# Cached keys turned by VectorE, longer runs of small tilings and 512-column memory matmuls in a streaming encoder step

## The chip, the cores and the metric

One core of one Trainium2 chip runs the whole step. The metric is the device time of one execution in microseconds; a kernel's time is the median of several runs. All data is float32. Most products are made in three passes: each operand is split into a high and a low part in a rounded float32 format (fp32r), and high x high, high x low and low x high are summed. Products with cached keys and values run on plain float32 operands, which the trace shows as two passes per matmul.

## The reference

Two layers over two groups of frames: a prompt of 512 frames, and 8 running streams of 16 frames each with a past of 256 (640 rows of 1024 in all).

```
m_l = rms_normalize(mem) * g_mem[l];  k, v = split(m_l @ w_x_kv[l])     # memory keys and values, 256 x 1024 each
layer 0:  q, k, v, f, gate = split(rmsnorm(x) @ w_fox_in)               # 16 heads of 64
          s = q k^T / 8 + cum(logf)_q - cum(logf)_k ; causal            # k, v: the cache, then the new rows
          x += ((softmax(s) v) * sigmoid(gate)) @ w_fox_out
layer 1:  c_q, c_kv, k_r = split(rmsnorm(x) @ w_mla_a)                  # latent of 256, rotary key of 32
          k_nope, v = split(c_kv @ w_kvb) ; s = (q_nope k_nope^T + q_rope k_r^T) * scale ; chunk mask
          x += (softmax(s) v) @ w_mla_out
each:     x += cross_attn(rmsnorm(x), k_mem, v_mem) ; x += swiglu(rmsnorm(x))
y = rmsnorm(x) * g_final
```

The outputs are y of both groups, the new keys, values and forget logs, the latents, the rotary keys and the memory keys and values.

## The kernel before

The phases follow each other: the first (Fox) attention, cross attention, feed-forward, the latent attention, cross attention, feed-forward. Each phase is written as lists of small steps, and `merge` interleaves several lists by their relative position, so that TensorE finds projections (a "fill" list) between the steps of an attention. A scheduler then orders the instructions on each engine, and engines work their queues in order. DMAs are issued by SyncE.

Weights come through `load_w`: a raw tile of 1024 columns (two buffers) is loaded, ScalarE rounds it into `whi` (L150), VectorE makes the rest `wlo` (L151), three buffers each.

The Fox phase runs over eight pairs of heads. `prompt_list` makes scores, softmax, transposed probabilities and values for the prompt. `sample_list` does it for the running streams in two halves `bq` of four streams: `load` fetches a tile `kr` of 128 x 8 x 128 cached keys (L654) and values `vr`, `keys` turns the keys by TensorE transposes into PSUM (L664, 16 per pair of heads) and VectorE or ScalarE copies them out (L668, L670), `scores` makes four matmuls in column tiles of 32 (L685), `trans` turns the probabilities, `values` makes twelve matmuls in the same tiling (L710), and `turn` brings the result to the output rows. In pairs 6 and 7 the fill is `mem_list`, the memory keys and values of both layers: per head and side 256 columns, two row tiles of 24 matmuls.

The latent phase absorbs the key weights into the queries (`turn_w`, L1488; `absorb`, L1498), then runs over eight pairs of heads of the prompt with the eight running streams spread among them: `keys` turns the cached latent (L1530) and the rotary key (L1535). `up_list` (L1588) takes the streams' results back to value space; `values` of the prompt (L1637) uses column tiles of 64. PSUM has two buffers for scores (`ps_s`), two for transposes (`ps_t`), one for values (`ps_o`) and three for projections (`mm`).

## Time and profile before

| | |
|---|---|
| median of 3 runs | 2115.81 us (2113.45 to 2122.21) |
| profiled execution | 2118.55 us, span 2116.8 us |
| TensorE busy | 2066.9 us, 98% |
| VectorE busy | 1393.1 us, 66% |
| ScalarE busy | 900.0 us, 43% |
| GpSimd busy | 176.0 us, 8% |
| DMA | 234.33 MB in 279279 packets |

The profiled execution is one run under the hardware profiler; its span runs from the first to the last instruction. Busy is the time in which at least one instruction of the engine was in work. Matmuls overlap each other in the array, so the duration of one is longer than its share of the queue.

### The profile page before, as it was taken

What the parts mean: (1) busy time and instruction counts of PE and PEld (TensorE: products, weight loads), DVE (VectorE), ACT (ScalarE), POOL (GpSimd) and SP (SyncE); (2) the same over time, 40 slices, a digit from 0 to 9 for tenths busy, and PEclk for the clock granted to TensorE, in tenths of its full rate; (3) what the DMA queues carried; (4) which work ended last, traced back from release to release, by engine and by line L of the source; (5) the groups of instructions that cost most, each with busy time, mean ns of one, the idle gap of its engine ahead of it and who ended that gap; (6) DMA issues with size and microseconds to landing.
All of it is one profiled execution on the core that took longest, in us unless ns stands there. A gap on an engine that the chain in (4) does not pass through costs nothing. (4 is left out here: it accounts for less than half of the span.)

```text
span 2116.8 us, 35888 instructions
## 1 busy us (share of the span) xinstructions
PE 2066.9 (98%) x14189; PEld 1857.4 (88%) x14189; DVE 1393.1 (66%) x2695; ACT 900.0 (43%) x1793; POOL 176.0 (8%) x362
## 2 busy tenths in 40 slices
PE   7999999999999999999999999999999999999998
PEld 7988888889987899999998978887887799999997
DVE  4454555564646796686686567767546896686686
ACT  4444444454443453343344455554443453343342
POOL 1121212120100000000001301100100000000000
PEclk9999999999999999999999999999999999999999
DMA  7443434477555322232221331112554322232221
GB/s 225 130 137 107 139 112 130 147 230 224 166 165 172 100 72 83 85 91 79 81 80 50 92 95 39 53 44 77 164 167 157 100 74 84 83 92 79 80 81 60
DMA packets 279279, 234.33 MB, mean 111 GB/s; under 512 B 15668, under 2 KB 255924, under 8 KB 279112
## 3 DMA queue, kind: packets, MB, share of 16 engines
q1 hardware_dynamic: 279112, 232.05, 36.0%
q8 instruction: 112, 1.84, 0.4%
q14 instruction: 55, 0.45, 0.1%
HBM read 214.80 MB, written 17.21 MB: 110 GB/s over the span
## 5 line engine op out<-in xcount | busy, mean ns | idle before, releaser
L204 PE MATMUL mm<-hT,whi 128*128 128x320 f32 x1744 | 291.5, 313 | 3.8 <-ACT hT L222 3.8
L204 PEld LDWEIGHTS mm<-hT,whi 128*128 128x128 f32 x1744 | 260.9, 188 | 9.8 <-ACT hT L222 5.2
L151 DVE TENSOR_TENSOR wlo<-raw,whi 128x1024 fp32r<-128x1024 f32 (+4 forms) x145 | 170.1, 1176 | 144.2 <-ACT whi L150 84.8
L318 DVE TENSOR_TENSOR X<-mm,X 128x512 f32<-128x512 f32 x270 | 182.8, 686 | 123.1 <-PE mm L204 121.8
L150 ACT CAST whi<-raw 128x1024 fp32r<-128x1024 f32 (+4 forms) x145 | 144.6, 1002 | 150.8 <-PE mm L204 103.4
L204 PE MATMUL mm<-whi,oT 128*128 128x512 f32 x544 | 182.9, 410 | 1.9 <-DVE X L318 1.1
L1103 ACT CAST whi<-tw 128x512 fp32r<-128x512 f32 (+1 forms) x120 | 91.9, 765 | 213.7 <-PE mm L204 127.5
L204 PE MATMUL mm<-whi,aT 128*128 128x512 f32 x560 | 173.0, 390 | 0.3 <-ACT aT L1068 0.3
L204 PE MATMUL mm<-hT,wlo 128*128 128x320 f32 x872 | 156.8, 312 | 0.0
L204 PEld LDWEIGHTS mm<-hT,wlo 128*128 128x128 f32 x872 | 133.4, 188 | 3.2 <-issue 3.1
L204 PE MATMUL mm<-whi,hT 128*128 128x256 f32 (+2 forms) x800 | 127.5, 298 | 2.4 <-ACT whi L150 1.5
L204 PE MATMUL mm<-s,whi 128*128 128x320 f32 x768 | 128.2, 309 | 0.0
L204 PEld LDWEIGHTS mm<-whi,aT 128*128 128x128 f32 x560 | 104.4, 188 | 22.6 <-ACT aT L1068 1.2
L232 POOL TENSOR_SCALAR rstd<-ss 128x1 f32<-128x1 f32 x49 | 17.2, 352 | 1266.0 <-ACT hn L230 1261.5
L204 PEld LDWEIGHTS mm<-whi,oT 128*128 128x128 f32 x544 | 96.6, 189 | 23.2 <-issue 3.7
L204 PEld LDWEIGHTS mm<-whi,hT 128*128 128x128 f32 x800 | 110.0, 193 | 7.7 <-issue 3.9
L204 PEld LDWEIGHTS mm<-s,whi 128*128 128x128 f32 x768 | 116.6, 188 | 0.0
L1104 DVE TENSOR_TENSOR wlo<-tw,whi 128x512 fp32r<-128x512 f32 (+1 forms) x120 | 103.4, 862 | 18.9 <-ACT whi L1103 18.4
L204 PE MATMUL mm<-wlo,oT 128*128 128x512 f32 x272 | 109.1, 401 | 0.0
L204 PE MATMUL mm<-wlo,aT 128*128 128x512 f32 x280 | 108.8, 389 | 0.0
L1103 ACT CAST whi<-raw 128x1024 fp32r<-128x1024 f32 x44 | 46.3, 1052 | 131.7 <-PE mm L204 72.3
L204 PE MATMUL ps_s<-whi,aT 128*128 128x512 f32 x320 | 98.6, 389 | 0.0
(340 smaller groups left out, 4280.5 us busy)
## 6 DMA issues: line engine op xcount, KB each, us to landing
rawg<-w_ffn_gu SPq DMA_DIRECT2D x80, 512.0 KB
raw<-w_ffn_down SPq DMA_DIRECT2D x44, 512.0 KB
raw<-w_x_kv SPq DMA_DIRECT2D x32, 512.0 KB
kr<-cache_mem_k SPq DMA_DIRECT2D x64, 256.0 KB
vr<-cache_mem_v SPq DMA_DIRECT2D x32, 512.0 KB
raw<-w_fox_in SPq DMA_DIRECT2D x30, 512.0 KB
kr<-cache_fox_k SPq DMA_DIRECT2D x16, 512.0 KB
vr<-cache_fox_v SPq DMA_DIRECT2D x16, 512.0 KB
```

Of the source, the lines that this page charges most:

```text
L150: A.copy(hi[:, 0:m], raw[:, 0:m])
L151: V.tensor_tensor(lo[:, 0:m], raw[:, 0:m], hi[:, 0:m].bitcast(F32), ALU.subtract)
L204: T.matmul(st["ps"][:, 0:n], lhsT=l, rhs=r, start=(j == 0), stop=(j == m - 1))
L232: G.tensor_scalar(r, ss, EPS, None, ALU.add)
L318: V.tensor_tensor(xs, ps, xs, ALU.add)
L1103: A.copy(hi[:, o:o + m], src)
L1104: V.tensor_tensor(lo[:, o:o + m], src, hi[:, o:o + m].bitcast(F32), ALU.subtract)
```

## The change

The cached keys are no longer transposed by TensorE. They are loaded in pieces of 32 columns onto 32 partitions each, so that a 32x32 block transpose on VectorE leaves them turned: four DMAs instead of one for each half pair in the Fox phase, and in the latent phase eight more per stream, which load the latent rows a second time (the first copy is still used as values). The new rows' key copy and the block mask of the probabilities move from VectorE to GpSimd. In the Fox phase both halves of the streams are scored and weighted in one step each; the prompt's last two query tiles of the latent phase share a score block, and its values and `up_list` are made in longer runs. The absorbed key weights are handled in full 128 rows, with the queries' other half set to zero. The memory keys and values are made 512 columns at a time, with the weights asked for in units of two row blocks, one unit ahead.

```diff
-        for h in range(4):
+        for c0 in range(0, D, 512):
             for i in range(2):
-                c0 = i * D + h * XD
                 u = {}
-                def load(u=u, c0=c0):
-                    u["w"] = load_w([(0, XD, w_kv[:, c0:c0 + XD])])
-                    u["row"] = pool().tile([P, 2, XD], F32, tag="mrow", name="mrow", bufs=2)
-                def store(u=u, i=i, h=h):
-                    S.dma_start(outs[i][:, :, h * XD:(h + 1) * XD], u["row"])
-                    S.dma_start(kvd[l][i].rearrange("(t p) n -> p t n", p=P)[:, :, h * XD:(h + 1) * XD], u["row"])
-                L = [load]
-                for t in range(2):
-                    L += gemm(lambda u=u, t=t: as_ops(d["mT"], slice(t * P, (t + 1) * P), u["w"], slice(0, XD), KD),
-                              XD, lambda ps, u=u, t=t: A.copy(u["row"][:, t, :], ps[:, 0:XD]), parts=2)
+                def load(m, u=u, c=i * D + c0):
+                    if m == 0:
+                        u["row"] = pool().tile([P, 2, 512], F32, tag="mrow", name="mrow", bufs=2)
+                    u[m] = load_w([(0, 512, w_kv[:, c:c + 512])], k0=2 * m, kt=2, per=2)
+                def part(m, u=u):
+                    for t in range(2):
+                        if m == 0:
+                            u["ps", t] = psum_mm()
+                        ops = [(d["mT"][ai][:, 2 * m + k, t * P:(t + 1) * P], u[m].get(wi, k))
+                               for wi, ai in PASSES for k in range(2)]
+                        for n, (l, r) in enumerate(ops):
+                            T.matmul(u["ps", t], lhsT=l, rhs=r, start=(m == 0 and n == 0), stop=(m == 3 and n == 5))
+                        if m == 3:
+                            A.copy(u["row"][:, t, :], u["ps", t])
+                def store(u=u, i=i, c0=c0):
+                    S.dma_start(outs[i][:, :, c0:c0 + 512], u["row"])
+                    S.dma_start(kvd[l][i].rearrange("(t p) n -> p t n", p=P)[:, :, c0:c0 + 512], u["row"])
+                L = [lambda load=load: load(0)]
+                for m in range(4):
+                    if m < 3:
+                        L.append(lambda load=load, m=m: load(m + 1))
+                    L.append(lambda part=part, m=m: part(m))
                 groups.append(L + [store])
...
-                    d["kr"] = fp.tile([P, 8, P], F32, tag="kr", name="kr", bufs=1)
-                    S.dma_start(d["kr"], ck[:, 8 * bq:8 * bq + 8, pr * P:(pr + 1) * P])
-                    d["vr"] = fp.tile([P, 8, P], F32, tag="vr", name="vr", bufs=2)
-                    S.dma_start(d["vr"], cv[:, 8 * bq:8 * bq + 8, pr * P:(pr + 1) * P])
-                    d["KT"] = fp.tile([P, 4, KS], F32, tag="KT", name="KT", bufs=2)
-                    V.tensor_copy(d["KT"][:, :, PAST:KS],
+                    kr = d["kr", bq] = fp.tile([P, 32, 32], F32, tag="kr", name="kr", bufs=2)
+                    for i in range(4):
+                        c0 = pr * P + 32 * i
+                        S.dma_start(kr[32 * i:32 * i + 32], ck[:, 32 * bq:32 * bq + 32, c0:c0 + 32])
+                    d["vr", bq] = fp.tile([P, 8, P], F32, tag="vr", name="vr", bufs=2)
+                    S.dma_start(d["vr", bq], cv[:, 8 * bq:8 * bq + 8, pr * P:(pr + 1) * P])
+                    d["KT", bq] = fp.tile([P, 4, KS], F32, tag="KT", name="KT", bufs=3)
+                    G.tensor_copy(d["KT", bq][:, :, PAST:KS],
                                   ks[pr][1][:, bq * 64:(bq + 1) * 64].rearrange("p (b t) -> p b t", t=TS))
-                def keys(b2):
-                    pt = psum_t()
-                    for i in range(4):
-                        T.transpose(out=pt[:, i * P:(i + 1) * P], in_=d["kr"][:, 4 * b2 + i, :], identity=ident)
-                    src = pt[:, :].rearrange("p (b t) -> p b t", t=PAST)
-                    dst = d["KT"][:, 2 * b2:2 * b2 + 2, 0:PAST]
-                    if b2 == 0:
-                        V.tensor_copy(dst, src)
-                    else:
-                        A.copy(dst, src)
-                def scores(bq):
-                    Q = qs_[pr][1]
-                    pw = d["pw"] = pw_tile()
+                def keys(bq, b2):
+                    V.transpose(d["KT", bq][:, 2 * b2:2 * b2 + 2, 0:PAST],
+                                d["kr", bq][:, 16 * b2:16 * b2 + 16, :].rearrange("p (b m) i -> p b (m i)", b=2))
+                def bias(bq):
+                    pw = d["pw", bq] = pw_tile()
...
+                def scores():
+                    Q = qs_[pr][1]
+                    sps = [psum_s() for _ in range(2)]
+                    for bq in range(2):
+                        for b in range(4):
+                            T.matmul(sps[bq][32 * b:32 * b + 32, 0:KS], lhsT=Q[:, 4 * bq + b, :],
+                                     rhs=d["KT", bq][:, b, :], start=True, stop=True, tile_position=(0, 32 * b))
+                    for bq in range(2):
+                        pw, sp = d["pw", bq], sps[bq]
+                        nm = small.tile([P, 1], F32, tag="nm", name="nm")
+                        V.tensor_tensor_reduce(out=pw[:, 0:KS], in0=sp[:, 0:KS], in1=pw[:, 0:KS], scale=-1.0,
+                                               scalar=3.0e38, op0=ALU.add, op1=ALU.min, accum_out=nm)
+                        ss = small.tile([P, 1], F32, tag="ssum", name="ssum")
+                        A.activation(pw[:, 0:KS], pw[:, 0:KS], AF.Exp, scale=-1.0, bias=nm, accum_out=ss)
+                        softmax_tail(pw, ss, KS)
+                        bm = cst[:, C_BM + P * bq:C_BM + P * (bq + 1)]
+                        G.tensor_tensor(pw[:, 272:400].rearrange("p (b t) -> p b t", t=TS),
...
                 def values():
                     op = psum_o()
-                    for kt in range(3):
-                        for b in range(4):
-                            rhs = d["vr"][:, 2 * b + kt, :] if kt < 2 else vs[g][:, TT - 1, cs_]
-                            T.matmul(op[32 * b:32 * b + 32, 0:P], lhsT=d["PT"][:, kt * P + 32 * b:kt * P + 32 * b + 32],
-                                     rhs=rhs, start=(kt == 0), stop=(kt == 2), tile_position=(0, 32 * b))
-                    d["osb"] = fp.tile([P, P], F32, tag="osb", name="osb", bufs=1)
-                    A.copy(d["osb"], op[:, 0:P])
-                def turn(bq):
+                    for bq in range(2):
+                        for kt in range(3):
+                            for b in range(4):
+                                rhs = d["vr", bq][:, 2 * b + kt, :] if kt < 2 else vs[g][:, TT - 1, cs_]
+                                T.matmul(op[32 * b:32 * b + 32, bq * P:(bq + 1) * P],
+                                         lhsT=d["PT", bq][:, kt * P + 32 * b:kt * P + 32 * b + 32],
+                                         rhs=rhs, start=(kt == 0), stop=(kt == 2), tile_position=(0, 32 * b))
+                    d["osb"] = fp.tile([P, 2, P], F32, tag="osb", name="osb", bufs=1)
+                    A.copy(d["osb"], op[:, 0:2 * P].rearrange("p (q n) -> p q n", q=2))
...
+                return [lambda: load(0), lambda: load(1)] + \
+                    [lambda bq=bq, b2=b2: keys(bq, b2) for bq in range(2) for b2 in range(2)] + \
+                    [lambda: bias(0), lambda: bias(1), scores, lambda: trans(0), lambda: trans(1), values, turn]
...
-                    qn = mp.tile([NOPE, 4, P], F32, tag="CT", name="qn", bufs=2)
-                    A.activation(qn, pq[0:NOPE, :].rearrange("p (h n) -> p h n", n=P), AF.Copy, scale=MLA_SCALE)
+                    qn = mp.tile([P, 4, P], F32, tag="CT", name="qn", bufs=2)
+                    G.memset(qn[NOPE:P], 0.0)
+                    A.activation(qn[0:NOPE], pq[0:NOPE, :].rearrange("p (h n) -> p h n", n=P), AF.Copy, scale=MLA_SCALE)
...
-                            T.transpose(out=pw_[0:NOPE, i * P:(i + 1) * P], in_=d["rv"][:, c, 2 * h2 + hh, 0:NOPE], identity=ident)
+                            T.transpose(out=pw_[:, i * P:(i + 1) * P], in_=d["rv"][:, c, 2 * h2 + hh, :], identity=ident)
...
-                    d["kr"] = mp.tile([P, 2, ROPE], F32, tag="krc", name="krc", bufs=2)
-                    S.dma_start(d["kr"], I["cache_mla_krope"][0, b].rearrange("(t p) c -> p t c", p=P))
+                    d["kr"] = mp.tile([ROPE, 8, ROPE], F32, tag="krc", name="krc", bufs=2)
+                    S.dma_start(d["kr"], I["cache_mla_krope"][0, b].rearrange("(m j) c -> j m c", j=32))
+                    d["cb"] = mp.tile([P, 2, 8, 32], F32, tag="cb", name="cb", bufs=2)
+                    src = I["cache_mla_ckv"][0, b].rearrange("(m j) (c i x) -> c i j m x", j=32, c=2, i=4)
+                    for c in range(2):
+                        for i in range(4):
+                            S.dma_start(d["cb"][32 * i:32 * i + 32, c], src[c, i])
                 def keys():
                     CT = d["CT"] = mp.tile([P, 2, KS], F32, tag="CT", name="CT", bufs=2)
                     KR = d["KR"] = KRs[b % 2]
-                    pt = psum_t()
-                    for c in range(2):
-                        for t in range(2):
-                            T.transpose(out=pt[:, c * 256 + t * P:c * 256 + (t + 1) * P], in_=cr[:, t, c * P:(c + 1) * P],
-                                        identity=ident)
-                    V.tensor_copy(CT[:, :, 0:PAST], pt.rearrange("p (c n) -> p c n", c=2))
-                    pt = psum_t()
-                    for t in range(2):
-                        T.transpose(out=pt[0:ROPE, t * P:(t + 1) * P], in_=d["kr"][:, t, :], identity=ident)
-                    A.copy(KR[0:ROPE, 0:PAST], pt[0:ROPE, 0:PAST])
+                    V.transpose(CT[:, :, 0:PAST], d["cb"].rearrange("p c m x -> p c (m x)"))
+                    V.transpose(KR[0:ROPE, 0:PAST], d["kr"].rearrange("p m x -> p (m x)"))
...
+                    for i in range(4):
+                        pr = 4 * u + i
+                        for c in range(2):
+                            for hh in range(2):
+                                T.matmul(po[64 * hh:64 * hh + 64, i * P:(i + 1) * P], lhsT=WV[:, c, 2 * pr + hh, :],
+                                         rhs=QA[c][:, :, 2 * pr + hh, :], start=(c == 0), stop=(c == 1))
+                    us = slice(4 * u, 4 * u + 4)
+                    evac_split(oTs[0][:, us, :], oTs[1][:, us, :], po.rearrange("p (i n) -> p i n", n=P))
+                return [lambda u=u: up(u) for u in range(2)]
...
+                for qts in ([3], [2], [1, 0]):
+                    L += [lambda qts=qts: scores(qts), lambda qts=qts: trans(qts)]
+                return L + [values]
```

What the scheduler makes of it is seen in the order of instructions. On TensorE, in the second pair of heads of the Fox phase, `kr` is the cached key tile, `vsb` the prompt's values, `oT` the attention output under projection and `hT` the normalised input. Before:

```order
L664 MATMUL ps_t<-cst,kr 128x128 x4
L638 MATMUL ps_o<-PT,vsb 64x128
L204 MATMUL mm<-whi,oT_1309 128x512
L204 MATMUL mm<-whi,oT_1310 128x512
L204 MATMUL mm<-wlo,oT_1309 128x512
L638 MATMUL ps_o<-PT,vsb 64x128 x13
L204 MATMUL mm<-whi,oT_1309 128x512
L204 MATMUL mm<-whi,oT_1310 128x512
L204 MATMUL mm<-wlo,oT_1309 128x512
L204 MATMUL mm<-hT_138,whi 128x320 x4
L204 MATMUL mm<-hT_139,whi 128x320 x4
L664 MATMUL ps_t<-cst,kr 128x128 x4
```

The same place after:

```order
L651 MATMUL ps_o<-PT,vsb 64x128 x3
L204 MATMUL mm<-whi,oT_1289 128x512
L204 MATMUL mm<-whi,oT_1290 128x512
L204 MATMUL mm<-wlo,oT_1289 128x512
L651 MATMUL ps_o<-PT,vsb 64x128 x11
L204 MATMUL mm<-whi,oT_1289 128x512
L204 MATMUL mm<-whi,oT_1290 128x512
L204 MATMUL mm<-wlo,oT_1289 128x512
L698 MATMUL ps_s<-KT,Qbd_97 32x272 x3
L204 MATMUL mm<-hT_138,whi 128x320 x4
```

Both groups of key transposes are gone, and the last three of the eight score matmuls (L698) stand apart from the first five, which come some twenty rows earlier. In the other pairs the eight are cut as five and three (pairs 2, 4 and 6) or one and seven (3, 5 and 7); in pairs 1 and 8 they stand together.

On VectorE, around the softmax of the running streams in the Fox phase (L688 before and L703 after is the row maximum with the bias, L330 and L331 the scaling). Before, in the second pair:

```order
L668 COPY KT<-ps_t 128x2x256
L642 TENSOR_TENSOR sig<-ps_o,sig 128x256
L679 ISA jk,cqs<-pw,cst 128x16
L679 ISA cqs 128x1
L658 COPY KT<-kn 128x4x16
L318 TENSOR_TENSOR X<-mm,X 128x512
L151 TENSOR_TENSOR wlo<-raw,whi 128x1024
```

After, in the second pair:

```order
L703 ISA pw,nm<-ps_s,pw 128x272
L703 ISA nm 128x1
L655 TENSOR_TENSOR sig<-ps_o,sig 128x256
L678 STREAM_TRANSPOSE KT<-kr 128x2x256
L318 TENSOR_TENSOR X<-mm,X 128x512
L330 RECIPROCAL rc<-ssum 128x1
L703 ISA pw,nm<-ps_s,pw 128x272
L703 ISA nm 128x1
L330 RECIPROCAL rc<-ssum 128x1
L678 STREAM_TRANSPOSE KT<-kr 128x2x256
```

Where the copy out of PSUM waited for TensorE, the transpose of the third pair's keys now stands among the steps of the two softmaxes and waits for a DMA.

## Rows read from the trace of the kernel before

**Rows 1.** The page: TensorE's busy time, and the DMA queue's packets, MB, share.

```profile
PE 2066.9 (98%) x14189; PEld 1857.4 (88%) x14189; DVE 1393.1 (66%) x2695; ACT 900.0 (43%) x1793; POOL 176.0 (8%) x362
...
q1 hardware_dynamic: 279112, 232.05, 36.0%
```

**Rows 2.** Windows: length, then busy us of PE, PEld, DVE, ACT, POOL; clock, DMA share, GB/s.

```profile
50.00:390.00 340.00, 339.58 (x2784) 300.29 (x2784) 180.68 (x496) 144.77 (x326) 66.64 (x138) 1.00 0.43 125
390.00:480.00 90.00, 84.75 (x739) 76.77 (x738) 54.27 (x109) 44.62 (x88) 18.85 (x34) 1.00 0.67 211
480.00:550.00 70.00, 66.34 (x522) 60.39 (x521) 42.24 (x68) 34.98 (x63) 9.24 (x15) 1.00 0.63 194
...
1235.00:1440.00 205.00, 201.38 (x1382) 170.11 (x1382) 147.47 (x391) 110.20 (x296) 19.48 (x50) 1.00 0.17 49
1440.00:1500.00 60.00, 55.79 (x369) 42.42 (x364) 46.33 (x89) 30.54 (x70) 7.68 (x13) 1.00 0.39 122
```

**Rows 3.** PE: key transposes (durations ns, first and last start us); memory matmuls (busy, mean).

```profile
L664 PE MATMUL ps_t<-cst,kr x128: 270/272/328, 71.5 to 490.9; 128*128 128x128 f32 x128
...
L204 PE MATMUL mm<-whi,mT 128*128 128x256 f32 x512 | 75.6, 289 | 0.3 <-ACT mT L222 0.3
```

**Rows 4.** Time line of PE in the Fox stage: start us, us, instruction, count.

```profile
117.05 0.60 PE L664 MATMUL ps_t<-cst,kr 128*128 128x128 f32 x4
117.40 1.20 PE L204 MATMUL mm<-whi,hT 128*128 128x256 f32 x8
118.44 0.64 PE L204 MATMUL mm<-wlo,hT 128*128 128x256 f32 x4
...
127.11 0.64 PE L204 MATMUL mm<-wlo,hT 128*128 128x256 f32 x4
127.67 0.67 PE L685 MATMUL ps_s<-KT,Qbd 128*32 128x272 f32 x8
128.27 1.22 PE L204 MATMUL mm<-whi,hT 128*128 128x256 f32 x8
129.32 0.64 PE L204 MATMUL mm<-wlo,hT 128*128 128x256 f32 x4
```

**Rows 5.** Time line of PE: memory matmuls of 256 columns, feed-forward matmuls of 512.

```profile
481.06 1.12 PE L204 MATMUL mm<-whi,mT 128*128 128x256 f32 x8
...
484.90 0.64 PE L204 MATMUL mm<-wlo,mT 128*128 128x256 f32 x4
...
1024.76 0.63 PE L204 MATMUL mm<-whi,aT 128*128 128x512 f32 x2
...
1029.32 0.39 PE L204 MATMUL ps_s<-wlo,aT 128*128 128x512 f32 x1
```

**Rows 6.** Time line of PE in the latent stage: an absorb block, the turned keys.

```profile
1214.84 1.16 PE L1498 MATMUL ps_s<-qn,PT 64*128 64x128 f32 x8
1215.92 1.08 PE L204 MATMUL mm<-whi,ckT 128*128 128x256 f32 x5
...
1402.06 0.60 PE L1530 MATMUL ps_t<-cst,H 128*128 128x128 f32 x4
1402.50 0.38 PE L1535 MATMUL ps_t<-cst,krc 128*32 128x128 f32 x2
1402.63 0.95 PE L218 MATMUL ps_s<-kT,qT 100*128 100x384 f32 x4
```

**Rows 7.** VectorE's copy of turned keys (busy, mean ns); SyncE's key loads (min/median/max ns).

```profile
L668 DVE COPY KT<-ps_t 128x512 f32<-128x512 f32 x16 | 10.9, 684 | 10.0 <-PE ps_t L664 10.0
...
L654 SPq DMA_DIRECT2D kr<-cache_fox_k x16: 367/374/509, 17.9 to 457.8; - x16
```

**Rows 8.** Waits of PE over the run: us in total, times, longest us.

```profile
PE ps_t L246 <- DVE hn L277: 9.3, 3, 8.7
...
PE ps_t L701 <- DVE pw L331: 1.7, 2, 1.5
...
PE ps_t L1622 <- DVE CT L1532: 0.6, 1, 0.6
```

More of the change, by code (lines that the diff above doesn't have):

```diff
@@ L699, in trans @@
+                def trans(bq):
                     pt = psum_t()
                     for i, o in enumerate((0, P, 272)):
-                        T.transpose(out=pt[:, i * P:(i + 1) * P], in_=d["pw"][:, o:o + P], identity=ident)
-                    d["PT"] = pt_tile()
-                    A.copy(d["PT"][:, 0:3 * P], pt[:, 0:3 * P])
+                        T.transpose(out=pt[:, i * P:(i + 1) * P], in_=d["pw", bq][:, o:o + P], identity=ident)
+                    d["PT", bq] = pt_tile()
+                    A.copy(d["PT", bq][:, 0:3 * P], pt[:, 0:3 * P])
@@ L716, in turn @@
+                    d["osb"] = fp.tile([P, 2, P], F32, tag="osb", name="osb", bufs=1)
+                    A.copy(d["osb"], op[:, 0:2 * P].rearrange("p (q n) -> p q n", q=2))
+                def turn():
                     pt = psum_t()
-                    T.transpose(out=pt[:, 0:P], in_=d["osb"], identity=ident)
-                    s0 = NP + 64 * bq
+                    for bq in range(2):
+                        T.transpose(out=pt[:, bq * P:(bq + 1) * P], in_=d["osb"][:, bq], identity=ident)
@@ L723, in turn @@
                                         sv, ALU.mult)
-                L = []
-                for bq in range(2):
-                    L += [lambda bq=bq: load(bq), lambda: keys(0), lambda: keys(1), lambda bq=bq: scores(bq),
-                          trans, values, lambda bq=bq: turn(bq)]
-                return L
+                return [lambda: load(0), lambda: load(1)] + \
+                    [lambda bq=bq, b2=b2: keys(bq, b2) for bq in range(2) for b2 in range(2)] + \
+                    [lambda: bias(0), lambda: bias(1), scores, lambda: trans(0), lambda: trans(1), values, turn]
@@ L776, in fox_phase @@
                 if pr == 6:
-                    fill += sum(mems[:7], [])
+                    fill += sum(mems[:4], [])
                 if pr == 7:
-                    fill += sum(mems[7:16], [])
+                    fill += sum(mems[4:9], [])
                 merge(prompt_list(pr), sample_list(pr), fill)
                 finish(pr)
-            for f in sum(mems[16:], []):
+            for f in sum(mems[9:], []):
                 f()
@@ L1580, in up_list, with up @@
             def up_list():
-                def up(pr):
-                    if pr == 0:
+                def up(u):
+                    if u == 0:
                         o = hpool.tile([P, 2, KD, P], F32R, tag="hT11", name="oTs", bufs=1)
@@ L1598, in prompt_list, with spans, scores @@
                 d = {}
-                def scores(qt):
-                    n = P * (qt + 1)
-                    qs = slice(qt * P, (qt + 1) * P)
-                    if qt == TT - 2 and j == 0:
+                def spans(qts):
+                    at, o = {}, 0
+                    for qt in qts:
+                        at[qt] = slice(o, o + P * (qt + 1))
+                        o += P * (qt + 1)
+                    return at, o
+                def scores(qts):
+                    at, _ = spans(qts)
+                    if TT - 2 in qts and j == 0:
                         oTf[g] = npool.tile([P, D], F32, tag="gb", name="oTf", bufs=1).rearrange("p (j n) -> p j n", j=2)
```

81 lines of the change are left out of this document (30 added, 51 removed).

## The prediction

> **What bounds the kernel now.** The page comes first: its busy times put TensorE at 98% of a span of 2116.8 us [rows 1]. The table by stages then says where that is literally true. In the stage of the first attention (50 to 390 us) TensorE is busy 339.58 of 340 us; while the memory keys and values are built (390 to 550) it idles 5.25 + 3.66 us; in the second half of the latent attention (1235 to 1500) it idles 3.62 + 4.21 us [rows 2]. VectorE, the next engine, has 180.68 of those 340 us. So every column that leaves TensorE's queue in these stages shortens the program, unless a wait appears in its place. The chain of waits can't tell more: TensorE's longest entry in it is 9.3 us, for the normalised rows between the stages, and those that this change touches are small ones [rows 8]. What is wanted, then, is the TensorE time of each edit, and that is read from start times in the time line, since the durations printed beside them overlap (four transposes "take" 0.60 us, yet the next row starts 0.35 us later [rows 4]).
>
> **The change part by part.** The sum is made against the profiled execution, 2118.55 us (its span of 2116.8 and 1.75 around it); the median of the three timed runs, 2115.81, lies 2.7 below, and I subtract the gain from the median.
>
> *Fox keys.* The 128 TensorE transposes of the cached keys go [rows 3], in 32 groups of four. They run from 71.5 to 490.9 us; with four groups to a pair of heads that is 31 steps, 54 us a pair. A group starts at 117.05 and the next row at 117.40: 0.35 us. The eight matmuls behind it then take 1.04 us (117.40 to 118.44 [rows 4]) where eight such take 8 x 0.120 = 0.96 [rows 5], so a group costs 0.43. 32 x 0.43 = **13.8 us**; bounds: 0.35 each (11.2) and 0.43 with the next row's 0.08 counted on both sides (16.3).
> The Trainium skill, VectorE: DVE Perf Modes, section The three transpose paths, gives 390 ns for a 128x128 transpose on TensorE (bf16) and 311 ns on VectorE. By that figure the 176 transposes of both attentions would free 68.6 us and the estimate would be near 2034; the rows show 0.11 us apiece in a queue, and the measurement decides.
>
> *What takes their place.* 32 VectorE transposes of 128x512. No row shows that instruction. From below, nothing (VectorE has 47% of the stage free); from above, twice the nearest row, the copy of the same shape out of PSUM, 684 ns [rows 7]. I take the 0.68 of that row: 32 x 0.68 = 21.9 us, less the 16 such copies that go (10.9), so under 1.5 us more per pair of heads even before the two small operations that move to GpSimd are taken off. ScalarE loses its 16 copies. GpSimd gets 32 short operations in a stage where it has 66.64 of 340 us [rows 2]. None of this lies on TensorE's path; if the cover went, it would be 11 us.
> The loads: a key load of 1024 packets becomes four with 4096 packets in all, of 128 bytes. SyncE issues 48 more, at 0.37 us [rows 7] 17.8 us of a queue that mostly waits. The packets have no row of their own; from below, they cost what their bytes cost (no more than now), from above as much as the mean packet of the run, 0.36 x 2116.8 x 16 / 279112 = 43.7 ns [rows 1], that is 11.2 us for a load and 22.4 for the two of a pair. The DMA engines are busy 43% of the stage [rows 2], 23.2 us of a pair's 54, of which the two old loads are at most 5.6: 40 of 54 at the upper bound. It fits, and the order shows the loads issued a pair ahead into two buffers, so I take 0.
>
> *Fox runs in the small tiling.* A run of four column tiles costs more than its work: the four matmuls ahead of it take 0.56 (127.11 to 127.67 [rows 4]) against 0.48, the eight behind it 1.05 against 0.96. So entering and leaving costs 0.17 us. The values become one run per pair of heads instead of two, 8 x 0.17 = 1.4. The scores were to do the same, but the order shows them cut in two again (five and three, one and seven) in six of eight pairs: 2 x 0.17 = 0.3. **1.7 us**, bounds 0 and 2.7.
>
> *Memory keys and values.* 768 matmuls of 256 columns (512 of the row shown [rows 3] and 256 with the low half of the weights) become 384 of 512. Between 481.06 and 484.90 stand 32 of the first kind: 0.120 us each. Between 1024.76 and 1029.32 stand 20 of the second: 0.228 [rows 5]. 92.2 - 87.6 = **4.6 us**. The weight conversions keep their number (32 units of 1024 columns), but are asked for one unit ahead of the matmuls instead of two at a time in front of them; of the idle 8.9 us of this stage that could give back half, and the two new PSUM tiles per group could cost as much. I take 0, bounds -4.5 and +4.5.
>
> *Latent keys.* Per sample the four transposes and the two of the rotary key stand between 1402.06 and 1402.63, 0.57 us [rows 6]: 8 x 0.57 = **4.6 us**, bounds 4 and 6. Eight DMAs more per sample (64 x 0.37 = 23.7 us of SyncE in a stage of 300) fetch the latent rows a second time.
>
> *Latent runs.* An absorb block of 64 rows takes 1.08 us for eight passes (1214.84 to 1215.92 [rows 6]); eight passes without a change of tiling, at the 0.11 of a transpose of as many columns, are 0.88. 8 x 0.2 = 1.6, and the transposes ahead of it, now 128 wide, lose a switch too, 8 x 0.08: **2.2 us**, bounds 0 and 4. Eight runs that bring the values up become two and sixteen runs of prompt values become eight: (6 + 8) x 0.17 = **2.4 us**, bounds 1 and 3.
>
> *Waits.* TensorE waited 0.6 us for the VectorE copy of the latent keys and 1.7 us for the sample softmax of the first attention [rows 8]. The first goes with the copy; the second I count as half gone, since both softmaxes of a pair now stand together and more work lies between scores and transposes. About **1.5 us**; below it, new waits of the same size.
>
> The sum: 13.8 + 1.7 + 4.6 + 4.6 + 2.2 + 2.4 + 1.5 = 30.8 us; 2115.8 - 30.8 = **2085 us**, 1.5% faster. The terms' own bounds, added up, give 15 to 43 us of gain, 2073 to 2101.
>
> **The rivals.**
> *The cover is lost.* The key transposes needed nothing but a DMA, so TensorE did them while VectorE and ScalarE worked at a softmax. Without them its queue is all matmuls with something to wait for, and half of the gain may come back as idle time, above all from 390 to 550 and 1235 to 1500 us, where it idles already. Against: between 50 and 390, where some 11 us of the gain lie, there are projections to do at every step, and TensorE idled 0.42 us. Half the gain: 2100.
> *More goes than the columns.* The latent stage has 7.8 us of waits in its second half, some of them at the short score blocks, which need one of two PSUM buffers back; joined in one block per pair they ask for it once less. With those waits and the upper bounds of the terms: 2068.
> *Slower: the small packets.* VectorE's queue is in order, and a key transpose now stands in it between the maximum and the scaling of a softmax. If its load is late, the softmaxes and evacuations behind it are late, and TensorE with them. That decides from (54 - 17.6) x 16 / 8192 = 71 ns per packet on: two loads of a pair then fill the DMA engines. At twice the mean packet's time, 87 ns, a pair needs 62.4 us and not 54: eight pairs, 67 us more, less the 13.8 us won in the memory and latent stages, 2169. For it: pieces a quarter as long, to 32 partitions at a time. Against: the mean packet of 831 bytes takes 43.7 ns, and these carry 128.
> The Trainium skill, DMA: Bandwidth & Descriptors, section Specifications, puts line rate at 512 bytes and more, with a read-modify-write below; that speaks for this rival, and I give it a few chances in a hundred more than the rows alone would. No row shows its price.
> *The change doesn't do what it says* in the score runs (seen above, 1.0 us already left out).
>
> **How the numbers follow.** The likeliest case, 0.62: 2073 to 2098. More goes: 0.13, 2060 to 2073. Cover lost: 0.17, 2098 to 2112, of which half lies within 0.5% of before (from 2105.2 on), about what a measurement of this kernel can tell from no change. Small packets or another new wait: 0.08, of which 0.05 slower by over 0.5% (2126.4) and the rest near no change. Range: 2064 to 2106, with some 0.04 left out below and 0.15 above. Faster 0.84, same 0.11, slower 0.05.
>
> **What would show it.** In the profile after: no transposes of cached keys on TensorE in either attention, TensorE's busy time down by about 30 us and its share of the span still 97% or more; the eight pairs of the first attention some 2 us shorter each and still without idle time up to the memory stage; a VectorE transpose of 128x512 at 0.5 to 0.7 us; 384 memory matmuls 0.23 us apart. Wrong would be: VectorE waiting for the key DMA, TensorE waiting for a softmax scale in the first stage, idle time in the memory stage above 9 us, or a share of the DMA engines near all of the first stage.

## The result, and the profile after

The changed kernel takes **2094.42 us** (median of 4 runs, 2093.67 to 2096.25) against 2115.89 (2113.45 to 2122.21): ratio 0.989 [0.9875, 0.9906], 1.1% faster. The forecast was 2085 us, between 2064 and 2106. The profiled execution took 2094.26 us, with a span of 2092.4.

The page of the changed kernel: busy us (share of the span) and instructions of each engine, and the DMA queue's packets, MB and share.

```profile
PE 2035.6 (97%) x13629; PEld 1818.6 (87%) x13629; DVE 1390.7 (66%) x2657; ACT 888.0 (42%) x1723; POOL 196.0 (9%) x398
...
q1 hardware_dynamic: 333896, 234.15, 38.7%
```

Beside [rows 1] this holds the whole case. TensorE's busy time fell by 31.3 us; the terms of the sum that are work make 29.3 (30.8 less the 1.5 of waits). The span fell by 24.4: idle time rose from 2116.8 - 2066.9 = 49.9 to 2092.4 - 2035.6 = 56.8 us. So the work as a whole was counted well, though not in each stage, and idle time took 6.9 us back. The windows say where (the same columns as [rows 2]; the stages now end sooner, so the later stretches are not the same work to the microsecond).

```profile
50.00:390.00 340.00, 335.36 (x2687) 293.15 (x2685) 187.88 (x487) 140.25 (x312) 82.52 (x167) 0.99 0.56 134
390.00:480.00 90.00, 85.67 (x515) 66.16 (x514) 52.47 (x97) 44.58 (x77) 21.00 (x40) 0.98 0.68 226
480.00:540.00 60.00, 56.37 (x337) 46.15 (x336) 37.94 (x59) 30.91 (x53) 8.55 (x13) 1.00 0.63 199
1220.00:1415.00 195.00, 188.69 (x1308) 163.13 (x1309) 142.92 (x388) 108.48 (x277) 19.02 (x49) 1.00 0.22 62
1415.00:1475.00 60.00, 55.53 (x380) 44.69 (x379) 44.78 (x84) 29.40 (x60) 9.33 (x13) 0.97 0.37 114
```

In the Fox stage, 50 to 390 us, TensorE idled 0.42 us and now idles 4.64: the one stage where it was never idle lost 4.2. The memory stage idles 4.33 + 3.63 us in 150, about as before (5.25 + 3.66 in 160). The latent stage lost nearly as much as the Fox stage. Between the same two steps of it (first matmul on the turned latent rows, last values of the prompt), before and then after (length, TensorE's busy us, clock, DMA share, GB/s):

```profile
1215.90:1475.30 259.40, 252.38 (x1732) 1.00 0.19 58
1202.90:1451.10 248.20, 237.56 (x1690) 1.00 0.24 67
```

TensorE idled 7.0 us there and now idles 10.6, 3.6 more; its work shrank by 14.8 us, where the terms for this stage make 9.2. In the rest of the run idle time fell by about 1 us. TensorE's waits of the Fox stage (us in total, times, longest us):

```profile
PE ps_t L636 <- DVE pw L331: 1.9, 1, 1.9
PE mm L204 <- DVE X L318: 1.2, 2, 1.0
PE ps_t L716 <- DVE pw L331: 0.9, 2, 0.5
PE ps_t L636 <- ACT PT L718: 0.3, 1, 0.3
```

L331 is the scaling of a softmax row by VectorE, ahead of the transposes of the prompt weights (L636) and the sample weights (L716). Only 0.9 us stand behind the softmax of the running streams. The longest wait, 1.9 us from 75.0 on, stands behind a softmax of the prompt and is over before the first sample scores of the phase start (92.3 us); 1.2 us go to VectorE's addition of an output block (L318). The new work itself is as small as was hoped. VectorE's transposes of the keys, with their durations (min/median/max ns), are those of the Fox keys, the latent keys and the rotary keys:

```profile
L678 DVE STREAM_TRANSPOSE KT<-kr x32: 668/695/711, 35.2 to 400.0; 128x512 f32<-128x512 f32 x32
...
L1550 DVE STREAM_TRANSPOSE CT<-cb x8: 703/711/714, 1220.4 to 1338.5; 128x512 f32<-128x512 f32 x8
...
L1551 DVE STREAM_TRANSPOSE KR<-krc x8: 412/414/426, 1152.5 to 1340.4; 32x256 f32<-32x256 f32 x8
```

The memory matmuls, from TensorE's time line: four of 512 columns start 0.91 us ahead of the next row, 0.228 apiece, as in [rows 5].

```profile
463.24 1.07 PE L374 MATMUL mm<-whi,mT 128*128 128x512 f32 x4
464.15 0.62 PE L374 MATMUL mm<-wlo,mT 128*128 128x512 f32 x2
```

In two of its eight pairs TensorE waits behind the softmax of the running streams, 0.4 to 0.5 us each time. This is the first of the two places. After both sample score blocks (L698) the two halves' softmaxes go through VectorE and ScalarE together; from the time line of the changed kernel:

```profile
189.53 1.12 PE L698 MATMUL ps_s<-KT,Qbd 128*32 128x272 f32 x14
...
190.35 0.44 DVE L703 CUSTOM_DVE_ANT_0 pw<-ps_s,pw 128x272 f32<-128x272 f32 x1
...
190.81 0.44 DVE L703 CUSTOM_DVE_ANT_0 pw<-ps_s,pw 128x272 f32<-128x272 f32 x1
...
191.34 1.05 ACT L150 CAST whi<-raw 128x1024 fp32r<-128x1024 f32 x1 [6.43 <-PE mm L204]
...
192.29 0.52 ACT L706 ACTIVATE pw<-pw,nm 128x272 f32<-128x272 f32 x1
192.42 1.22 DVE L151 TENSOR_TENSOR wlo<-raw,whi 128x1024 fp32r<-128x1024 f32 x1 [0.16 <-ACT whi L150]
...
193.56 0.21 DVE L330 RECIPROCAL rc<-ssum 128x1 f32<-128x1 f32 x2
...
194.03 0.63 DVE L331 TENSOR_SCALAR pw<-pw,rc 128x272 f32<-128x272 f32 x2
...
194.44 0.92 PE L716 MATMUL ps_t<-cst,pw 128*128 128x128 f32 x3 [0.44 <-DVE pw L331]
```

From the first maximum (190.35) to the scaling (194.03) pass 3.7 us. The first exponential starts 1.94 us after the first maximum: a weight conversion (1.05) stands ahead of it in ScalarE's queue, which had itself waited for TensorE until 191.34, when the second maximum was done. Then the conversion's second half (1.22) stands on VectorE ahead of the reciprocals. TensorE has had its transposes next in the queue since 194.0 and waits 0.44.

### The profile page after: what moved, and what is told of

It reads as the page before. It is cut to its first block, busy times and chain, and to the rows that moved or that the text cites. A ratio compares the mean times of both kernels' runs of the same rounds, so it can differ in the third digit from the quotient of the medians.

```text
span 2092.4 us, 34811 instructions
## 1 busy us (share of the span) xinstructions
PE 2035.6 (97%) x13629; PEld 1818.6 (87%) x13629; DVE 1390.7 (66%) x2657; ACT 888.0 (42%) x1723; POOL 196.0 (9%) x398
## 2 busy tenths in 40 slices
DMA packets 334059, 236.37 MB, mean 113 GB/s; under 512 B 99124, under 2 KB 298420, under 8 KB 333896
## 3 DMA queue, kind: packets, MB, share of 16 engines
q1 hardware_dynamic: 333896, 234.15, 38.7%
## 5 line engine op out<-in xcount | busy, mean ns | idle before, releaser
L318 DVE TENSOR_TENSOR X<-mm,X 128x512 f32<-128x512 f32 x270 | 183.5, 686 | 121.7 <-PE mm L204 120.0
L204 PEld LDWEIGHTS mm<-whi,aT 128*128 128x128 f32 x560 | 104.4, 188 | 23.3 <-ACT aT L1083 1.9
```

The costliest lines, as they stand in the source:

```text
L204: T.matmul(st["ps"][:, 0:n], lhsT=l, rhs=r, start=(j == 0), stop=(j == m - 1))
L318: V.tensor_tensor(xs, ps, xs, ALU.add)
```

## The experiments

The kernels ran in three groups of four, each group on one chip; ratios are to the kernel before on that chip (medians 2119.23, 2117.86 and 2118.61 us).

| kernel | median us (range) | ratio [95%] | TensorE busy, idle us | busy in 50:390 | first memory matmul at us |
|---|---|---|---|---|---|
| before | 2115.89 (2113.5 to 2122.2) | 1 | 2066.9, 49.9 | 339.58 | 398.4 |
| after | 2094.42 (2093.7 to 2096.3) | 0.9890 [0.9875, 0.9906] | 2035.6, 56.8 | 335.36 | 389.4 |
| Fox part alone (first group) | 2108.93 (2107.4 to 2113.3) | 0.9957 [0.9939, 0.9974] | 2052.0, 53.7 | 334.39 | 389.2 |
| memory part alone | 2114.5 (2112.5 to 2119.4) | 0.9981 [0.9970, 0.9991] | | | |
| latent part alone | 2110.94 (2108.2 to 2112.3) | 0.9959 [0.9945, 0.9973] | | | |
| after, one set of transposes put back | 2100.37 (2098.6 to 2105.5) | 0.9915 [0.9895, 0.9935] | 2045.1, 54.8 | 338.05 | 392.8 |
| after, two sets put back (second group) | 2114.37 (2110.9 to 2118.1) | 0.9983 [0.9974, 0.9992] | 2058.1, 54.4 | 337.56 | 403.6 |
| after, sample part in halves | 2091.26 (2089.6 to 2095.8) | 0.9878 [0.9866, 0.9891] | 2035.6, 52.1 | 338.74 | 385.5 |
| after, memory norms earlier | 2099.8 (2095.8 to 2105.9) | 0.9917 [0.9903, 0.9931] | | 334.18 | |
| after, 64-byte loads | 2089.55 (2089.4 to 2091.3) | 0.9869 [0.9856, 0.9881] | | 336.26 | 387.5 |
| control: after again (third group) | 2093.55 (2090.4 to 2094.8) | 0.9879 [0.9864, 0.9894] | 2035.0, 53.6 | 334.80 | 389.0 |
| halves, one set put back | 2100.72 (2100.6 to 2103.6) | 0.9918 [0.9903, 0.9933] | 2048.1, 53.7 | 337.29 | 397.8 |
| halves for the scores, values joined | **2086.9** (2086.6 to 2088.8) | **0.9852** [0.9837, 0.9866] | 2035.6, 48.9 | 338.74 | 385.6 |
| halves, 64-byte loads | 2093.26 (2091.2 to 2095.8) | 0.9884 [0.9867, 0.9900] | | | |

The last three columns are of the profiled execution, the last the first start of a matmul on the memory rows, thus the length of everything up to there. The changed kernel's two profiled executions differ by 3.8 us in span and by 0.4 us at that point. Of the 9.0 us between before and after there, 3.2 lie ahead of the Fox stage, whose first transposes of new key rows start at 50.4 us before and at 47.2 after:

```profile
L512 PE MATMUL ps_t<-cst,krow x32: 271/273/329, 50.4 to 338.5; 128*128 128x128 f32 x32
...
L525 PE MATMUL ps_t<-cst,krow x32: 271/273/328, 47.2 to 331.5; 128*128 128x128 f32 x32
```

That is at most in part the change's doing: with the memory part or the latent part alone, whose Fox stage is the old one, they start at 48.4 and 48.8.

**The parts alone.** The edits of the diff, applied to the kernel before in three groups. Their first lines:

```
 the Fox part alone
-                def keys(b2):
+                def keys(bq, b2):
...
 the memory part alone
-        for h in range(4):
+        for c0 in range(0, D, 512):
...
 the latent part alone
+                    V.transpose(CT[:, :, 0:PAST], d["cb"].rearrange("p c m x -> p c (m x)"))
...
```

> The Fox part alone on the kernel before (keys turned by VectorE, both halves of the streams in one step), the rest unchanged. Columns theory (a removed transpose is worth its queue time): 15 us faster than before, near 2101. Cover theory (the transposes filled time in which TensorE would have waited): about half, 2108. Small packets: no gain, 2116 or more.

> The memory keys and values alone in 512 columns, on the kernel before. Columns theory: 5 to 7 us faster, near 2110. If the waits that the trace after shows in this stage (2.3 us behind the normalised memory rows, 1.3 us for a row buffer, and a half clock after one of them) belong to this edit: 2 us or less, 2114 to 2116.

> The latent part alone on the kernel before. Columns theory: 9 to 11 us faster, 2105 to 2107. If the merged score blocks and the single run of values add waits: 5 us or less, 2111 or more. The three parts should add up to the 21.5 us of the whole if they don't hinder each other.

Out of 2117 us the ratios give 9.1 us for the Fox part, 4.0 for the memory part and 8.7 for the latent part, 21.8 in all against 23.3 for the whole: the parts add up. The Fox part came at the time expected if the cover is lost (2108), the memory part between its two cases, the latent part just short of the first of its two. Against the terms of the sum the memory part (4.6 forecast) came as worked out, and the latent part's 8.7 is near its 9.2 and 0.6 of waits. What is missing is in the Fox part, 9.1 where the terms for its keys and runs and most of the waits made about 16.

The latent part came near by two errors that cancel. Its profiled execution has 13.5 us less busy time than the kernel before (2053.4), not 9.2, and 2.8 us more idle time (52.7), not 0.6 less. Counted from each matmul's start to the next one's, idle time left out, the largest piece that no term has is the score matmuls of the prompt, whose last two query tiles now share a block: 37.8 us of the stage before, 33.6 with the latent part and 33.7 in the changed kernel. The same joined blocks bring a new wait; in the changed kernel (time line, and the waits from 1165 to 1480 us):

```profile
1247.37 0.47 ACT L1642 ACTIVATE hn<-ps_s,nm 128x256 f32<-128x256 f32 x1 [1.15 <-DVE nm L1640]
...
1248.41 0.37 ACT L1642 ACTIVATE hn<-ps_s,nm 128x128 f32<-128x128 f32 x1 [0.48 <-DVE nm L1640]
...
1249.02 1.16 PE L1559 MATMUL ps_s<-CT,H 128*128 128x272 f32 x4 [2.44 <-ACT hn L1642]
...
PE ps_s L1559 <- ACT hn L1642: 3.4, 5, 2.4
```

The scores of a stream (L1559) wait for one of the two score buffers until ScalarE has done both exponentials (L1642) of a joined block. The same wait of 3.4 us stands in the latent part alone; in the kernel before no stream's scores wait for the prompt's exponentials.

**The Fox transposes put back, unread.** In the changed kernel, behind each VectorE transpose; the output is unchanged.

```
+                    pt = psum_t()
+                    for i in range(4):
+                        T.transpose(out=pt[:, i * P:(i + 1) * P],
+                                    in_=d["kr", bq][:, 16 * b2 + 4 * i:16 * b2 + 4 * i + 4, :].rearrange("p m i -> p (m i)"),
+                                    identity=ident)
```

> The changed kernel with the 128 TensorE transposes of the Fox keys put back as extra work: they read the newly loaded key tiles into a PSUM tile that nobody reads; VectorE still makes the turned keys. The output is unchanged. Columns theory: 12 to 14 us slower than the changed kernel, 2107. Cover theory: the transposes fill waits and cost half or less, 2098 to 2101.

They cost 5.3 us by the ratios (7.6 from the control's ratio), 6 to 7 by the medians (2100.37 against 2094.42 and 2093.55), about half of what their start times say. Four of them at 122.72 us still move the next row by 0.36 us (123.08), and the Fox stage around them shows that they stand where TensorE else waits:

```profile
50.00:390.00 340.00, 338.05 (x2785) 301.03 (x2784) 184.42 (x478) 136.04 (x308) 76.52 (x167) 1.00 0.55 132
```

Idle time there is 1.95 us and not 4.64. From each transpose's start to the next matmul's the set itself takes 12.8 us of the queue. The profiled execution is only 7.5 us longer than the changed kernel's: over the run it idles 2.0 us less, and it has one stretch of 3.4 us at half clock between start and end where the changed kernel has three, an estimated 3.4 us of work. Against the control's profiled execution the gap is 11.3 us, so one execution alone does not settle how much was covered.

**The same twice over**, with the loop over `2 * list(range(4))`.

> The changed kernel with the 128 transposes of the Fox keys put back twice over (256 in all, into a PSUM tile that nobody reads; the VectorE transposes stay, the output is unchanged). One set cost 4 to 5 us where its start times say 11 to 14. If the first set only filled waits of TensorE, the second set finds none left and costs its full 32 x 0.35 to 0.43, 11 to 14 us: 15 to 18 us above the changed kernel, ratio 0.996 to 0.998. If a transpose is simply cheaper in the queue than its start times say, the second set costs what the first did: 8 to 10 us above, ratio 0.993 to 0.994.

2114.37, 14.0 us above one set (on another chip; 14.4 by the ratios), the first result of the two expected, though one set had cost 5 us or more and not the 4 to 5 that this starts from. TensorE's busy time rose by 13.0 us and its idle time stayed (54.8 and 54.4). A set of 128 transposes is worth its 32 x 0.43 = 13.8 us as soon as nothing is left to fill; the price of the term was right, and the first set was partly paid for by time that was lost without it.

**The sample part in halves**, as before the change, with the keys on VectorE (the steps are written here without their lambdas; `scores(bq)` begins with `bias(bq)`).

```
-    [lambda bq=bq, b2=b2: keys(bq, b2) for bq in range(2) for b2 in range(2)] + \
-    [lambda: bias(0), lambda: bias(1), scores, lambda: trans(0), lambda: trans(1), values, turn]
+    for bq in range(2):
+        L += [load(bq), keys(bq, 0), keys(bq, 1), scores(bq), trans(bq), values(bq), turn(bq)]
```

> The changed kernel, with the sample part of the first attention in two halves again (own scores, softmax, values and turn for each half, as before), while its cached keys are still turned by VectorE. It tells which part of the Fox edit makes the new waits. If the removed transposes alone took the cover away, the two halves cost only the eight joined runs, 0 to 2 us more than the changed kernel: ratio to the kernel before 0.989 to 0.990. If the waits come from the joined softmaxes (two score blocks through VectorE at once), this kernel is 2 to 5 us faster than the changed one: 0.987 and below, and the waits of 74.7, 180 and 281.5 us are gone.

Inconclusive by the time alone: the ratio is the control's (0.9878 and 0.9879), the medians are 2.3 us apart on two chips. In the stage it is not: the memory matmuls begin at 385.5 us and not at 389.4 and 389.0, so the joined sample part costs 3.5 to 3.9 us up to there where it was forecast to bring 1.7 and a part of 1.5. The difference is idle time: from 50 to 390 us TensorE idles 1.26 us and not 4.64 or, in the control, 5.20. TensorE's only waits above 0.15 us in the stage are these:

```profile
PE ps_s L697 <- DVE nm L620: 0.5, 2, 0.3
PE mm L374 <- ACT mT L222: 0.2, 1, 0.2
```

**The memory norms one group earlier**: `mems = m0[:4] + [m1[0], m0[4]] + m1[1:]`.

> The changed kernel with the memory norms of the second layer one group earlier (before the last key-value group of the first layer, not right ahead of the first group that needs them). The changed kernel waits 2.3 us for the turned memory rows at 449 us and runs 3.4 us at half clock behind it. If the wait goes with the order, 2 to 4 us faster than the changed kernel: ratio 0.987 to 0.988. If the last wait there is another one (weight conversions on ScalarE and VectorE), no change: 0.989.

A miss: 2099.8 us, some 6 slower than the control by the medians (on another chip). The mean granted clock from 390 to 540 us is 0.95, and 0.99 in the changed kernel. TensorE's waits from 390 to 540 us show that the wait only changed its place, and a longer one came behind it, for ScalarE's copy of the sample weights:

```profile
PE ps_t L636 <- ACT PT L718: 4.3, 1, 4.3
PE ps_t L246 <- DVE hn L238: 3.1, 2, 2.6
```

**Smaller packets.** Eight DMAs a load, of 64-byte pieces, instead of four.

```
-    S.dma_start(kr[32 * i:32 * i + 32], ck[:, 32 * bq:32 * bq + 32, c0:c0 + 32])
+    for x in (0, 16):
+        S.dma_start(kr[32 * i:32 * i + 32, :, x:x + 16], ck[:, 32 * bq:32 * bq + 32, c0 + x:c0 + x + 16])
```

> The changed kernel with each key load of the first attention in eight DMAs of 64-byte packets in place of four of 128 bytes: twice the packets (16384 a pair), the same bytes. The changed trace has 13 ns for the median 128-byte packet: the packets added are 8192 x 13 / 16 = 6.7 us of the DMA engines a pair of some 53, which are busy 56% now. Columns and cover theory: no change, 0.988 to 0.990. If the price of the small packets is part of what is missing in the Fox gain: slower by 3 us or more, 0.9905 and above, with VectorE waiting for the key loads.

Not slower, if anything faster (0.9869, the intervals overlap the changed kernel's and the control's). The DMA engines' share of the Fox stage rises from 0.56 to 0.65 and the packets from 333896 to 400456:

```profile
q1 hardware_dynamic: 400456, 234.16, 40.3%
...
50.00:390.00 340.00, 336.26 (x2706) 292.60 (x2705) 188.93 (x488) 141.24 (x313) 82.35 (x170) 1.00 0.65 133
```

The packet time of all 16 engines is 0.387 x 2092.4 x 16 = 12956 us after and 0.403 x 2089.5 x 16 = 13473 here: 517 us for 66560 packets more, 7.8 ns each.

**Transposes put back into the halves**, the control, and the joined values alone:

> The kernel with the sample part in halves (2091 us) with one set of the 128 TensorE transposes of the Fox keys put back, as was done to the changed kernel, where it cost 4 to 6 us. If the transposes had only filled waits that any softmax leaves (the rival that the cover is lost), it costs 4 to 6 us here too: 2095 to 2098, ratio 0.989 to 0.991. If the waits come from the joined sample softmax and not from the missing transposes, then nothing is there to fill and the set costs its full 11 to 14 us: 2102 to 2106, ratio 0.993 to 0.9945.

> The changed kernel itself, as the control for the three kernels of this chip: 2093 to 2097 us, ratio 0.989 to 0.990.

> Of the joined sample part only the values and their turn stay joined; scores and softmax are in two halves. If the joined scores make the waits (two score blocks, then two softmaxes, one behind the other on VectorE and ScalarE), this kernel has the halves' 2091 us and the saved runs of the values besides (8 x 0.17 = 1.4): 2089 to 2091, ratio 0.987 to 0.9875. If the joined values make them (they need both halves' weights), it stands at the changed kernel's 2094 to 2097.

The set costs 9.5 us in the halves by the medians (8.5 by the ratios) and 12.3 up to the first memory matmul (385.5 to 397.8); in the changed kernel it was 5.3 to 7.6, and 3.4 to 3.8 up to there. Of its 32 groups 26 stand ahead of that point in the halves and 28 in the changed kernel, 11.2 and 12.0 us at 0.43 each. Up to there, then, the set has its full price in the halves and a third of it in the changed kernel: it fills idle time that the joined sample part made (4.64 to 1.95 us in 50:390), and none in the halves (1.26 to 2.71). The 12.3 also hold that added idle time and a stretch of 3.4 us at half clock (54.2 us) that the halves alone don't have. By the medians the cost falls between the two results expected, so some of the cover, behind 390 us, may belong to the removal itself; runs of these two kernels scatter by 3 to 6 us, and this stays open.

The third kernel undoes the joining of all that stands ahead of the values: each half has its own loads, key transposes, bias, scores, softmax and weight transposes again.

```
-    [lambda: bias(0), lambda: bias(1), scores, lambda: trans(0), lambda: trans(1), values, turn]
+    for bq in range(2):
+        L += [load(bq), keys(bq, 0), keys(bq, 1), scores(bq), trans(bq)]
+    L += [values, turn]
```

It takes 2086.9 us, 6.7 below the control on the same chip, with no run in common (2086.6 to 2088.8 against 2090.4 to 2094.8), below both results expected, and is the fastest kernel here. Its page and its windows have the changed kernel's busy time to the tenth, in a span of 2084.5 us:

```profile
PE 2035.6 (98%) x13629; PEld 1820.9 (87%) x13629; DVE 1388.3 (67%) x2657; ACT 886.7 (43%) x1723; POOL 196.5 (9%) x398
...
50.00:390.00 340.00, 338.74 (x2725) 296.79 (x2724) 191.19 (x493) 141.86 (x317) 89.14 (x179) 1.00 0.57 133
```

The whole difference of the profiled executions is idle time, 48.9 us and not 56.8 (53.6 in the control). In the time line the same softmax as above, now of one half:

```profile
186.28 1.05 ACT L150 CAST whi<-raw 128x1024 fp32r<-128x1024 f32 x1 [4.97 <-PE mm L204]
...
187.25 0.44 DVE L702 CUSTOM_DVE_ANT_0 pw<-ps_s,pw 128x272 f32<-128x272 f32 x1
...
189.44 0.32 DVE L331 TENSOR_SCALAR pw<-pw,rc 128x272 f32<-128x272 f32 x1
```

2.2 us from maximum to scaling and not 3.7, with work of TensorE behind it: ScalarE began its weight conversion before the maximum. The run shows what the joining ahead of the values costs, not which of the joined steps costs it: the loads, keys and biases move with the scores, and with the shorter list every step of the sample part stands elsewhere in the merged order. That it also beats the halves by 4 us (another chip) is more than the 1.4 of the joined value runs; both reach the memory stage at the same time (385.6 and 385.5), so this difference isn't in those runs, and its cause stays open.

> The sample part in halves together with the 64-byte key loads. The 64-byte loads alone stood at 2089.6 us and the halves alone at 2091.3, on another chip than the changed kernel's 2094.4. If the smaller packets bring something of their own, both together give 2086 to 2088, ratio 0.985 to 0.986; if that was a difference of chips or of where waits happen to fall, 2089 to 2092, ratio 0.987 to 0.988.

2093.26, the control's time, just above the second result expected: 64-byte packets bring nothing of their own here. That the 2089.55 of the group before was a matter of the chip or of where its waits fell is the reading that is left; it was not tried.

## Why the prediction was right, point by point

- **TensorE sets the end: held.** Busy time fell by 31.3 us for 29.3 of work in the sum, and the share is 97%. One row was misread, without harm to the sum: of the 9.3 us that the prediction puts between the stages, 8.7 are the start of the run, ahead of TensorE's first transpose at 8.7 us.
- **Fox keys, 13.8 us: the price held, the cover did not.** A set costs 14.0 where nothing is idle; in the changed kernel it costs 5 to 8 to put back, because part of it fills time that is lost without it.
- **Fox runs in the small tiling, 1.7 us, and waits, 1.5: the steps that failed.** The prediction said that "both softmaxes of a pair now stand together and more work lies between scores and transposes", and took a gain from it. It costs instead: with the joining ahead of the values undone the kernel is 6.7 us faster, 3.4 of them up to the memory stage. TensorE waiting for a softmax scale in the first stage was one of the prediction's own signs of being wrong, and it came (1.9 and 0.9 us). How the joining costs is shown in part only. Directly behind the joined softmax stand 0.9 us of wait. For the rest the trace offers the order of the steps: TensorE has no sample matmuls for the first part of each pair, and the first come at 92.3 us, where the halves have theirs at 74.2. That this is why the 1.9 us of L636 (75.0 us) and the 1.0 of L318 (180 us) are not covered is argued from the trace and was not tried apart.
- **"The cover is lost": the rival that came nearest, at another place.** It was put at 390 to 550 and 1235 to 1500 us. The first kept its idle time; the second has 3.6 us more, but what waits longest there is a stream's scores for a buffer held by a joined score block of the prompt, and that is not shown to have to do with the removed transposes. The Fox stage, where "there are projections to do at every step", lost 4.2 us. A stage with 0.42 us of idle time in 340 has no slack that is known: that its waits are covered was true with the work that was then taken out.
- **Eight pairs 2 us shorter each: failed.** From the first transposes of new key rows to the first memory matmul, 26 of the 32 groups of key transposes or six and a half pairs, the changed kernel is 5.8 us shorter (348.0 to 342.2), 0.9 a pair. With the joining ahead of the values undone it is 9.5 us (338.5), 1.5 a pair.
- **Memory 4.6: held**, 4.0 measured. In the changed kernel the stretch from the first to the last memory matmul is 3.5 us shorter (398.4 to 523.4 before, 389.4 to 510.9). With the memory part alone it is 125.0 us as before, 6.8 of them at half clock, so where its 4.0 us lie in that run stays open.
- **Latent 4.6 + 2.2 + 2.4 + 0.6: the time held, 8.7 measured, but by luck.** The work fell by 13.5 and not 9.2, with 4.2 us in the prompt's score matmuls that no term has, and idle time rose by 2.8 where 0.6 was to go. The rival "More goes than the columns" expected the joined score blocks to ask for a buffer once less and wait less; a stream's scores wait 3.4 us for them.
- **Work moved to VectorE: held.** 0.695 us a transpose against the 0.68 taken; VectorE's busy time of the run is 1390.7 us for 1393.1. The Trainium skill, VectorE: DVE Perf Modes, section The three transpose paths, has 311 ns for a 128x128 bf16 transpose in blocks of 32x32; here a 128x512 one in f32 takes 695 ns, 174 for each 128 columns, so its figure is not the price here.
- **Small packets: dead.** Halving them once more cost 7.8 ns for each added packet and no time. The line rate of 512 bytes and more that the Trainium skill, DMA: Bandwidth & Descriptors, section Specifications, states did not matter, since 44% of the engines' time was free.

The time came out 9 us above the forecast. Of that, 6.7 are the joining ahead of the values; with it undone the ratio is 0.9852, which on the 2115.8 us of the time before is 2084.5, the sum's 2085. That the two meet so closely is luck in part, since the latent stage is right by errors that cancel.

## What to carry to other kernels

Where one engine is busy all of a stage, count its busy time and its idle time apart: the first can be summed from rows, the second belongs to the order of the steps, and work that waits for nothing pays for part of itself. Joining two short runs saves a switch, 0.17 us by the prediction's rows, and moves every step ahead of it to another place in the order; here joining loads, scores and softmaxes cost more than it saved, while joining the values behind them did no harm. A total that comes out right can hide two errors: compare busy and idle time stage by stage. To find how much of a removed job was cover, put it back unread once and then twice: the second set shows its price and the first what it covered.

## What the runs showed of the hardware

The granted clock falls to half for 3.4 us at a time in the midst of a busy stage, often right behind a short wait. Windows of the changed kernel, TensorE's busy us, clock, DMA share, GB/s:

```profile
73.60:77.00 3.40, 1.49 (x11) 0.99 0.03 3
77.00:80.40 3.40, 3.40 (x15) 0.50 0.18 38
80.40:83.80 3.40, 3.40 (x25) 1.00 0.95 282
449.00:452.40 3.40, 1.24 (x7) 1.00 0.30 83
452.40:455.80 3.40, 3.40 (x13) 0.50 0.96 333
```

Waits of 1.9 and 2.2 us stand in the first and fourth row; TensorE was at 2.4 GHz in them and at 1.2 GHz in the full stretch behind. At half the clock 3.4 us do the work of 1.7, an estimate, so such a wait can cost nearly its own length again. Of the kernel before, the only such stretch between the start and the last microseconds lies at 35.7 us.

A wait is neither enough for it nor needed. The control, the same kernel, waits 1.9 us at the same place and keeps the full clock (first two rows); the halves with one set put back run at half clock from 54.2 us on after a stretch in which TensorE was busy throughout (last two):

```profile
73.24:76.64 3.40, 1.84 (x13) 1.00 0.13 12
76.90:80.30 3.40, 3.36 (x26) 1.00 0.27 64
50.80:54.20 3.40, 3.40 (x29) 1.00 0.87 182
54.20:57.60 3.40, 3.40 (x16) 0.50 0.12 23
```

What decides it is not shown here.
